# All input projections of a hybrid encoder layer in the first stage, the local attention between the steps of the scans, and the blocks of tokens taken middle first

## The chip, the cores and the metric

One core of one Trainium2 chip runs the whole layer in one launch. The metric is the device time of that launch in microseconds (us), the median over several runs. TensorE (PE in the rows) does the matrix products, VectorE (DVE), ScalarE (ACT) and GpSimd (POOL) the rest, and SyncE (SP) issues nearly all DMAs.

## The reference

One encoder layer on 2048 tokens of width 1024, in fp32. The normalised input goes through one projection whose columns feed three groups of heads; their outputs are joined and projected, and cross attention and a feed-forward layer follow.

```python
h = rmsnorm(x, norm_mix_w[l])
(na_q, na_k, na_v, ml_q, ml_k, ml_v, ml_o, ml_i, ml_f,
 gd_q, gd_k, gd_v, gd_z, gd_b, gd_a) = jnp.split(h @ w_in[l], IN_OFFSETS, axis=-1)
y_na = neighbourhood_attention(...)   # 6 heads of 64, windows of 8 x 16 on a 32 x 64 grid
y_ml = mlstm_mixer(...)               # 4 heads of 64, a scan over chunks in each direction
y_gd = gated_deltanet_mixer(...)      # 6 heads of 64, convolution, a scan in each direction
x = x + jnp.concatenate([y_na, y_ml, y_gd], axis=-1) @ w_out[l]
x = x + memory_cross_attention(rmsnorm(x, norm_xa_w[l]), rmsnorm(mem, norm_mem_w[l]), ...)
x = x + jnp.square(jax.nn.relu(rmsnorm(x, norm_ffn_w[l]) @ w_ff1[l])) @ w_ff2[l]
```

## The kernel before

Tokens go in four blocks of 512, activations lie transposed (features on partitions). A product with a weight tile of 128 columns (`gemm`, L1021, through `mm3`, L102) is 24 matmuls of 512 columns: eight slices of the 1024 features, each three times, since both operands are split into a high and a low part. I call such 24 matmuls a group. A weight tile is made by `wtile` (L980): a DMA of 512 KB, a rounding copy on ScalarE (L987, `whi`) and a subtraction on GpSimd (L989, `wlo`). The input projections are 120 groups: 36 for the delta rule's q, k, v (`gdn_in`, nine tiles per block), 4 for the gates, 24 for the mLSTM's q, k, v (`ml_in`), 32 for the attention's keys and values and the mLSTM's output gate (`na_kv`), 12 for the attention's queries (`na_q`), 12 for the delta rule's output gate (`gdn_z`).

The program is written as generators that a fixed order interleaves. A scheduler then arranges the instructions of each engine's queue; once built, each engine works through its queue in order. The stages are:

- **First stage** (`pass_a`, 0 to about 835 us). For each block: the nine tiles of `gdn_in`, each followed by a convolution over five tokens on VectorE (L299 to L311); then `gates`, and for each pair of chunks of 64 tokens `gram` (Gram matrices, decays, operands of the scan to DRAM). `inv` inverts the triangular matrices group by group: thirty pairs of VectorE instructions per direction (L495, L496), then rounds of small products (L524). Between these stand the mLSTM's projections and some of `na_kv`. Only two normalised blocks fit (`acta`, `actb`).
- **Scans** (`pass_b`, about 835 to 1290 us). The delta rule (`gdn_scan`, L653 to L689) and the mLSTM (`ml_scan`, L838 to L898), 16 steps each, both directions at once, with operands from DRAM loaded one step ahead. After each step one group of the projections that are left (`rest`) is put in. Blocks 0 and 1 have to be normalised again for this (`renorm`).
- **Attention** (`pass_c`, about 1290 to 1612 us). Sixteen blocks of 8 x 16 queries, six heads each (`na`, L948 to L976): scores, a bias and a maximum on VectorE (L952), exponentials on ScalarE (L953), transposes on TensorE (L957), the product with the values (L967). Scores take two banks of PSUM (`psn`), transposes two others (`pst`). The last projections and the other heads' outputs (`heads_out`, L707 to L727) stand between the blocks; the last five blocks stand between the tiles of the output projection's first block (`mixed`).
- **Rest**: output projection, cross attention, feed-forward layer.

The table below sets how many groups or steps go between two pieces; the line after it, in `pass_b`, is the place at which projections stand between the steps of the scans.

```python
B_FILL = 1
C_FILL = 3
NA_LATE = 11
OUTS = (0, 0, 0, 0, 1, 3, 3, 3, 3, 3, 0)
...
                    self.step(rest, B_FILL, L_B)
```

## Time and profile before

| | us |
|---|---|
| median of 3 runs | 3795.64 |
| the three runs | 3795.94, 3795.64, 3775.17 |
| span of the profiled execution, first to last instruction | 3789.0 |
| TensorE busy in the span | 3468.7 |
| VectorE busy | 1819.1 |
| GpSimd busy | 1601.0 |
| ScalarE busy | 1153.2 |

For the profiled execution only its span is known, 3789.0 us; two of the three timed runs lie 6.6 and 6.9 us above it, the third 13.8 us below. Busy time counts an instruction for as long as it runs, so TensorE's busy time is also longer where its clock is lower: the profile has a column with the clock granted to TensorE, where 1.00 is 2.4 GHz and 0.50 is 1.2 GHz. A busy time multiplied by the granted clock is what the same work would take at full clock; I call that warm work.

### The profile page before, as it was taken

To read this page: it belongs to the slowest core of one execution; us is meant where nothing else is said; L and a number is where in the kernel's file an instruction comes from. 1 tells how busy PE (TensorE), PEld (TensorE's weight loads), DVE (VectorE), ACT (ScalarE), POOL (GpSimd) and SP (SyncE) were. 2 spreads that over 40 slices of the span, in tenths; PEclk is the share of its full clock that TensorE was granted. 3 is DMA by queue.
4 is the path that set the end of the run, shared out by engine and by line. 5 is a ranking of instruction groups with operands and counts; after the bars stand their busy time and mean duration, and the time that the engine had idled before them with its cause. 6 is when DMAs were issued, how large, how long until landed. Compare 5 with 4: busy or idle time off the path is not lost.

```text
span 3789.0 us, 54073 instructions
## 1 busy us (share of the span) xinstructions
PE 3468.7 (92%) x21392; PEld 2774.0 (73%) x21392; DVE 1819.1 (48%) x3257; ACT 1153.2 (30%) x2015; POOL 1601.0 (42%) x947
## 2 busy tenths in 40 slices
PE   5878688888788889999999999999999999999998
PEld 4656566666666655588888887888888778888887
DVE  7697977625666644553443436222222352222224
ACT  3233232232323333544343344222222332222223
POOL 4455444554454531253535445333333453333333
PEclk9988888988899996999999999999999999999999
DMA  4546475678999565742233233111111141111112
GB/s 140 179 132 183 140 193 142 174 181 200 202 215 217 173 216 172 210 174 98 95 134 134 87 123 133 53 45 48 45 50 48 60 138 48 49 53 48 53 47 89
DMA packets 396663, 466.07 MB, mean 123 GB/s; under 512 B 151978, under 2 KB 296826, under 8 KB 393338
## 3 DMA queue, kind: packets, MB, share of 16 engines
q1 hardware_dynamic: 392794, 450.55, 41.2%
q0 software_dynamic: 3616, 12.06, 0.9%
q8 instruction: 169, 2.77, 0.3%
q14 instruction: 84, 0.69, 0.1%
HBM read 360.01 MB, written 102.50 MB: 122 GB/s over the span
## 4 chain that ended last, share of the span: by engine, by line
PE 52%; DVE 1%; ACT 1%; issue 1%; DMA 0%; POOL 0%; POOLq 0%; DVEq 0%; SPq 0%; ACTq 0%
PE psg L108 31%; PE psa L108 21%; PE psa L1180 0%; DVE nh L1005 0%; DVE ss L1016 0%; PE psm L88 0%; PE psm L99 0%; ACT whi L987 0%; DMA out_y<-nh 0%; DMA xb<-x_d 0%; POOL wlo L989 0%; DVE xb L1251 0%; ACT acta L1137 0%; ACT acta L1006 0%; ACT sqt L1015 0%
## 5 line engine op out<-in xcount | busy, mean ns | idle before, releaser
L989 POOL TENSOR_TENSOR wlo<-wraw,whi 128x1024 fp32r<-128x1024 f32 (+2 forms) x401 | 842.0, 2101 | 1294.1 <-ACT whi L987 1271.7
L108 PE MATMUL psg<-acta,whi 128*128 128x512 f32 x3008 | 975.3, 404 | 36.9 <-ACT pad L295 23.2
L108 PE MATMUL psg<-actb,whi 128*128 128x512 f32 (+2 forms) x2752 | 857.4, 393 | 36.8 <-DVE rt L613 10.2
L987 ACT CAST whi<-wraw 128x1024 fp32r<-128x1024 f32 (+2 forms) x417 | 373.5, 896 | 1192.3 <-PE psa L108 551.7
L108 PEld LDWEIGHTS psg<-acta,whi 128*128 128x128 f32 x3008 | 576.7, 194 | 169.2 <-ACT pad L295 25.2
L108 PE MATMUL psa<-ht,whi 128*128 128x512 f32 x2048 | 638.6, 395 | 0.6 <-ACT whi L987 0.5
L108 PEld LDWEIGHTS psg<-actb,whi 128*128 128x128 f32 (+1 forms) x2752 | 518.9, 193 | 148.2 <-ACT pad L295 11.2
L108 PE MATMUL psg<-acta,wlo 128*128 128x512 f32 x1504 | 602.5, 402 | 3.6 <-POOL wlo L989 3.6
L108 PE MATMUL psg<-actb,wlo 128*128 128x512 f32 (+2 forms) x1376 | 539.9, 393 | 27.9 <-POOL wlo L989 27.9
L108 PEld LDWEIGHTS psa<-ht,whi 128*128 128x128 f32 x2048 | 384.0, 188 | 95.1 <-ACT whi L987 1.5
L1229 DVE TENSOR_TENSOR fr<-fr 128x512 f32<-128x512 f32 x128 | 167.9, 1312 | 495.4 <-ACT fr L1228 495.4
L1242 DVE TENSOR_TENSOR xb<-psa,xb 128x512 f32<-128x512 f32 x256 | 175.6, 691 | 476.4 <-PE psa L108 476.3
L108 PE MATMUL psa<-ht,wlo 128*128 128x512 f32 x1024 | 401.0, 396 | 0.7 <-POOL wlo L989 0.7
L108 PEld LDWEIGHTS psg<-acta,wlo 128*128 128x128 f32 x1504 | 290.8, 193 | 67.6 <-POOL wlo L989 5.0
L108 PEld LDWEIGHTS psg<-actb,wlo 128*128 128x128 f32 (+1 forms) x1376 | 265.2, 193 | 86.5 <-POOL wlo L989 33.4
L1232 POOL TENSOR_TENSOR ht<-fr,ht 128x512 fp32r<-128x512 f32 x128 | 169.1, 1321 | 249.1 <-ACT ht L1231 247.8
L108 PEld LDWEIGHTS psa<-ht,wlo 128*128 128x128 f32 x1024 | 192.3, 188 | 47.5 <-POOL wlo L989 1.8
L1016 DVE TENSOR_TENSOR ss<-ss,sqt 128x512 f32<-128x512 f32 (+1 forms) x91 | 123.4, 1356 | 47.0 <-ACT sqt L1015 44.3
L308 DVE SCALAR_TENSOR_TENSOR acc<-pad,vecs,acc 128x512 f32<-128x512 f32 (+2 forms) x144 | 143.6, 1000 | 1.5 <-DVE sm L436 0.6
L1231 ACT CAST ht<-fr 128x512 fp32r<-128x512 f32 x128 | 79.4, 621 | 180.1 <-DVE fr L1229 180.0
L1228 ACT ACTIVATE fr<-psg 128x512 f32<-128x512 f32 x128 | 75.9, 593 | 132.3 <-PE psg L108 132.3
L495 DVE TENSOR_TENSOR tv<-x 72x30 f32<-72x30 f32 (+36 forms) x210 | 94.4, 470 | 2.0 <-DVE x L496 0.6
(376 smaller groups left out, 3982.3 us busy)
## 6 DMA issues: line engine op xcount, KB each, us to landing
wraw<-in_w_ff SPq DMA_DIRECT2D x72, 512.0 KB
wraw<-in_w_ff SPq DMA_DIRECT2D x144, 256.0 KB
wraw<-in_w_gd SPq DMA_DIRECT2D x36, 512.0 KB
sc_d<-sc SPq DMA_DIRECT2D x32, 576.0 KB
xt<-in_xT SPq DMA_DIRECT2D x16, 1024.0 KB
wraw<-in_w_out SPq DMA_DIRECT2D x32, 512.0 KB
wraw<-in_w_xq SPq DMA_DIRECT2D x32, 512.0 KB
wraw<-in_w_xo SPq DMA_DIRECT2D x32, 512.0 KB
```

The lines of the kernel that those rows point to most:

```text
L108: nc.tensor.matmul(out=out, lhsT=a(k), rhs=b(k), start=(i == 0), stop=(i == n - 1))
L308: V.scalar_tensor_tensor(out=acc[:, :n], in0=pad[:, p0 + j:p0 + j + n], scalar=cw(j), in1=acc[:, :n], op0=ALU.mult, op1=ALU.add)
L495: V.tensor_tensor(out=tv, in0=m[:, j + 1:32, j:j + 1].broadcast_to([2 * N, n, j]), in1=m[:, j:j + 1, 0:j].broadcast_to([2 * N, n, j]), op= ...
L987: nc.scalar.copy(out=hi, in_=raw)
L989: (lo_eng or nc.gpsimd).tensor_tensor(out=lo, in0=raw, in1=hi.bitcast(F32), op=ALU.subtract)
L1016: nc.vector.tensor_tensor(out=ss, in0=ss, in1=sq, op=ALU.add)
L1228: S.activation(out=r, in_=ps, func=AF.Relu)
L1229: V.tensor_tensor(out=r, in0=r, in1=r, op=ALU.mult)
L1231: S.copy(out=ht[:, 0], in_=r)
L1232: G.tensor_tensor(out=ht[:, 1], in0=r, in1=ht[:, 0].bitcast(F32), op=ALU.subtract)
L1242: V.tensor_tensor(out=xs[nb][:, j], in0=ps, in1=xs[nb][:, j], op=ALU.add)
```

## The change

All 120 groups of projections now stand in the first stage, which works on pairs of blocks: each weight tile of the pair is made once and used for both blocks (the first few tiles of `gdn_in`, `LEAD`, excepted, which are made for each block). Nothing is normalised twice. The scans' stage holds no projection any more: after each step stand three pieces (one block) of the attention, and from the tenth round on two pieces of `heads_out`, which now begins with the tokens in the middle, since both directions of the scans have passed them first. The attention's scores and transposes share two banks of PSUM (`psn`), and `heads_out` shares two with the mLSTM's scan (`psl`). The weights' and activations' memory (`gemm_pools`) is freed after the first stage, used by the attention and by `heads_out`, and taken anew for the rest. There the blocks go in the order 1, 2, 0, 3; the memory's norm and its first four tiles of keys stand ahead of the output projection, which no longer overlaps with the attention. Comments have gone, so line numbers differ by 8 to 19: the scans' L653, L672, L679, L686 are now L640, L659, L666, L673; the mLSTM's L849, L853, L878, L885 are L837, L841, L866, L873; the attention's L948, L957, L967, L972 are L936, L945, L955, L962; the heads' transposes L723 are L710; the projections' L108 is L95.

```diff
+LEAD = (4, 2)
+ORDER = (1, 2, 0, 3)
+KV_FIRST = 4
...
+            self.norm_in(1)
+            for pr in range(2):
+                bs = (2 * pr, 2 * pr + 1)
+                n = LEAD[pr]
+                for ct, blocks in [(c, bs[:1]) for c in range(n)] + [(c, bs) for c in range(n, 9)] + [(c, bs[1:]) for c in range(n)]:
+                    w = self.wtile(self.I["w_gd"][ct], KT, "w")
+                    for b in blocks:
+                        self.gdn_in(b, ct, w)
+                for b in bs:
+                    self.gates(b)
+                fill = chain(self.ml_in(bs), self.na_kv(bs), self.na_q(bs), *(self.gdn_z((b,)) for b in bs)) if pr == 0 else chain(self.na_kv(bs), self.na_q(bs), self.ml_in(bs), self.gdn_z(bs))
...
+            attn = self.na(pool("na", 2, side="right"))
             scan = self.gdn_scan(pool("scan", 2))
+            out = self.heads_out(pool("out", 2, side="right"))
...
+            for m in range(16 + LAG):
+                next(scan, None)
+                if m >= LAG:
+                    next(ml)
+                self.step(attn, 3)
+                if m - LAG >= 8:
+                    self.step(out, 2)
+            for _ in chain(attn, out):
+                pass
...
-        for t in range(16):
-            yield
+        yield
+        for t in (7, 8, 6, 9, 5, 10, 4, 11, 3, 12, 2, 13, 1, 14, 0, 15):
...
-                    tp = self.ntp.tile([P, 512], F32, name="pst")
+                    tp = self.nps.tile([P, 512], F32, name="psn")
...
-        blocks = sorted(NA_BLOCKS)
+        blocks = sorted(NA_BLOCKS, key=lambda k: (ORDER.index(k[0]), k[1]))
```

The first place is TensorE's queue in the middle of the scans. Before, a step of the delta rule (`pss`) and of the mLSTM (`psl`) has matmuls of the projections (`psg`, operands `acta`, `actb` and the weights' `whi`, `wlo`) in between.

```order
L885 MATMUL psl<-mr__10267,msc 64x65 x8
L653 MATMUL pss<-wp,kb 64x64 x24
L849 MATMUL psl<-mkq 64x64 x8
L853 MATMUL psl<-ident,mkq 64x128 x3
L672 MATMUL pss<-sc,wp 64x64 x12
L853 MATMUL psl<-ident,mkq 64x128
L108 MATMUL psg<-acta,wlo 128x512
L108 MATMUL psg<-acta,whi 128x512 x2
L108 MATMUL psg<-actb,whi 128x512
```

In the changed kernel a step looks like this, with the attention's scores and transposes (`psn`) and its products with the values (`psy`).

```order
L866 MATMUL psl<-mr__11299,msc 64x65 x8
L659 MATMUL pss<-sc,wp 64x64
L945 MATMUL psn<-ident,nas 96x128 x3
L945 MATMUL psn<-ident,nas 72x128
L936 MATMUL psn<-nak,naqb 128x360
L659 MATMUL pss<-sc,wp 64x64 x11
L873 MATMUL psl<-mr__11299,msc 64x65 x8
L866 MATMUL psl<-mr__11299,msc 64x65 x8
L955 MATMUL psy<-nap,nav 64x128
L666 MATMUL pss<-sc 64x64
L673 MATMUL pss<-sc 64x64
```

The projections have left this place, and every head's transposes (L945) now stand directly ahead of the next head's scores (L936).

The second place is TensorE's queue at the end of the attention. Before, matmuls of the output projection (`psg`) follow between its last heads.

```order
L948 MATMUL psn<-nak,naqb 128x288
L967 MATMUL psy<-nap,nav 64x128
L972 MATMUL pst<-ident,nsm 64x128 x6
L948 MATMUL psn<-nak,naqb 128x288
L967 MATMUL psy<-nap,nav 64x128 x5
L957 MATMUL pst<-ident,nas 96x128 x3
L948 MATMUL psn<-nak,naqb 128x288
L108 MATMUL psg<-acta,whi 128x512 x3
L108 MATMUL psg<-acta,wlo 128x512
```

In the changed kernel the attention is through by then; the last three steps of the mLSTM (`psl` from `msc`) and the last heads' transposes (`psl` from `ob`) stand alone, then come the memory's norm (`psm`) and the first product of the rest.

```order
L841 MATMUL psl<-ident,mkq 64x128 x4
L866 MATMUL psl<-mr__13869,msc 64x65 x8
L873 MATMUL psl<-mr__13869,msc 64x65 x8
L866 MATMUL psl<-mr__13869,msc 64x65 x8
L873 MATMUL psl<-mr__13869,msc 64x65 x8
L710 MATMUL psl<-ident,ob 128x128 x10
L866 MATMUL psl<-mr__14238,msc 64x65 x8
L873 MATMUL psl<-mr__14238,msc 64x65 x16
L710 MATMUL psl<-ident,ob 128x128 x10
L76 MATMUL psm<-ones,ss 128x1 x2
L86 MATMUL psm<-ident,rs 128x128 x2
L95 MATMUL psg<-actb,whi 128x256 x2
```

No dense product is left between the last heads; the first one of the rest stands behind all of them.

## Rows read from the trace of the kernel before

**Rows 1.** The page: span and busy time of TensorE and VectorE.

```profile
span 3789.0 us, 54073 instructions
...
PE 3468.7 (92%) x21392; PEld 2774.0 (73%) x21392; DVE 1819.1 (48%) x3257; ACT 1153.2 (30%) x2015; POOL 1601.0 (42%) x947
```

**Rows 2.** Busy time by stage, granted clock, DMA share (first stage, scans, attention).

```profile
core 0: us, PE busy (x) PEld busy (x) DVE busy (x) ACT busy (x) POOL busy (x), PEclk, DMA share, GB/s
0.00:835.00 835.00, 666.30 (x4456) 524.25 (x4457) 634.65 (x1287) 252.33 (x358) 412.36 (x219) 0.88 0.59 162
835.00:1290.00 455.00, 365.74 (x5375) 299.84 (x5373) 275.50 (x529) 134.12 (x259) 222.58 (x154) 0.90 0.87 204
1290.00:1612.00 322.00, 298.31 (x1768) 190.27 (x1768) 160.51 (x500) 133.31 (x359) 91.07 (x48) 0.86 0.64 198
```

**Rows 3.** The same stretches, the projections' matmuls (L108) alone.

```profile
0.00:835.00 835.00, 541.89 (x2032) 403.52 (x2033) 0.88 0.59 162
835.00:1290.00 455.00, 163.25 (x579) 112.10 (x577) 0.90 0.87 204
1290.00:1612.00 322.00, 73.86 (x285) 56.05 (x285) 0.86 0.64 198
```

**Rows 4.** The chain of waits: start, us, what; a group of 24 at full clock.

```profile
1907.14 5.49 PE psg L108 x24
```

**Rows 5.** Busy time by stretch: start, convolutions, twice Gram matrices with projections.

```profile
0.00:43.00 43.00, 16.18 (x53) 12.42 (x54) 23.81 (x43) 17.55 (x28) 19.87 (x24) 1.00 0.60 193
43.00:116.00 73.00, 56.33 (x231) 42.80 (x230) 67.87 (x97) 25.82 (x34) 33.03 (x14) 0.86 0.37 109
430.00:514.00 84.00, 64.24 (x340) 52.34 (x341) 64.19 (x157) 17.26 (x24) 36.63 (x13) 0.84 0.55 147
600.00:700.00 100.00, 89.71 (x842) 73.23 (x841) 65.60 (x162) 29.98 (x46) 41.44 (x20) 0.86 0.76 206
```

**Rows 6.** VectorE's groups in the first stage: busy us, mean ns, idle before.

```profile
L308 DVE SCALAR_TENSOR_TENSOR acc<-pad,vecs,acc 128x512 f32<-128x512 f32 (+2 forms) x144 | 143.6, 1000 | 1.5 <-DVE sm L436 0.6
L259 DVE TENSOR_REDUCE ss<-sq 128x256 f32<-128x1024 f32 x16 | 31.4, 1963 | 9.6 <-ACT sq L258 9.6
L311 DVE SCALAR_TENSOR_TENSOR acc<-th,acc 128x512 f32<-128x512 f32 (+2 forms) x36 | 30.0, 833 | 3.2 <-ACT th L310 3.1
L306 DVE TENSOR_SCALAR acc<-pad,vecs 128x512 f32<-128x512 f32 (+2 forms) x36 | 19.9, 552 | 3.8 <-DMA gd_c<-acc 2.9 <-ACT pad L295 0.8
L299 DVE COPY pad<-edge 128x4 f32<-128x4 f32 x27 | 19.2, 710 | 0.1
L303 DVE COPY edge<-pad 128x4 f32<-128x4 f32 x27 | 18.5, 685 | 3.2 <-ACT pad L295 3.1
```

**Rows 7.** Groups of instructions: VectorE's norm, attention's heads, heads' outputs on GpSimd.

```profile
L266 DVE SCALAR_TENSOR_TENSOR xt<-xt,vecs,psm 128x256 f32<-128x256 f32 x120 | 48.8, 471 | 33.0 <-PE psm L99 20.7 <-DMA xt<-in_xT 12.2
L948 PE MATMUL psn<-nak,naqb 64*128 64x360 f32 (+5 forms) x192 | 82.3, 594 | 0.1
L957 PE MATMUL pst<-ident,nas 128*96 128x128 f32 (+1 forms) x336 | 61.6, 308 | 3.6 <-ACT nas L953 2.7 <-ACT nay L974 0.9
L953 ACT ACTIVATE nas<-nas,nam 128x360 f32<-128x360 f32 (+5 forms) x96 | 57.8, 603 | 48.2 <-DVE nam L952 36.8 <-PE psm L723 3.5 <-DVE hss L715 3.4
L952 DVE CUSTOM_DVE_ANT_0 nas<-psn,nab 128x360 f32<-128x360 f32 (+5 forms) x96 | 51.1, 538 | 56.2 <-PE psn L948 50.0 <-PE pst L957 5.7
L707 POOL TENSOR_TENSOR ob<-ob 128x640 f32<-128x640 f32 x16 | 24.7, 1542 | 147.4 <-DMA ob<-ho_d 119.2 <-PE psn L948 18.8 <-PE pst L957 4.5
```

**Rows 8.** Ten-microsecond stretches of the attention: a wait, then a lower clock.

```profile
1370.00:1380.00 10.00, 10.00 (x72) 7.19 (x69) 3.80 (x14) 3.10 (x10) 3.40 (x2) 1.00 0.60 193
1410.00:1420.00 10.00, 7.06 (x41) 3.79 (x38) 4.76 (x20) 5.18 (x16) 4.99 (x3) 0.83 0.83 249
1420.00:1430.00 10.00, 10.00 (x40) 5.42 (x39) 3.22 (x11) 1.70 (x5) 1.95 (x1) 0.50 0.65 188
...
1450.00:1460.00 10.00, 9.72 (x73) 5.94 (x72) 6.16 (x19) 5.72 (x17) 3.46 (x2) 0.97 0.70 208
```

More of the change, by code (lines that the diff above doesn't have):

```diff
@@ L1 @@
 from contextlib import ExitStack
-from itertools import chain
+from itertools import chain, islice
 import numpy as np
@@ L167, in pass_a @@
             self.zero_w()
[L168 removed]
+            self.edges = [self.gp.tile([P, 9, 4], F32, name=f"edge{i}") for i in range(3)]
             with self.tc.high_priority(offset=500):
                 self.norm_in(0)
[L171 to L192 removed]
@@ L193, in pass_a @@
-            for _ in inv:
-                self.step(rest, I_FILL, L_A)
-        self.sp = None
-    def step(self, gen, n, late=0):
-        with self.tc.high_priority(offset=-late):
-            for _ in range(n):
-                next(gen, None)
-    def pass_b(self, rest):
+            self.norm_in(1)
[9 more added lines that the diff above has]
+                fill = chain(self.ml_in(bs), self.na_kv(bs), self.na_q(bs), *(self.gdn_z((b,)) for b in bs)) if pr == 0 else chain(self.na_kv(bs), self.na_q(bs), self.ml_in(bs), self.gdn_z(bs))
+                if pr == 0:
+                    self.grams((0, 1, 2), fill)
+                    inv = self.inv(0, (0, 1))
+                    self.steps(inv, fill, I_FILL, 1)
+                    self.grams((3, 4, 5, 6), fill)
+                    self.steps(chain(inv, self.inv(1, (0, 1))), fill, I_FILL)
+                    self.steps(fill, iter(()), 0, 34 - 14)
+                    self.norm_in(2)
+                    self.steps(fill, iter(()), 0)
+                    self.norm_in(3)
+                else:
+                    self.grams((15, 14, 13, 12, 11), fill)
+                    inv = self.inv(3, LAST[0])
+                    self.steps(inv, fill, I_FILL, 1)
+                    self.grams((7, 8, 9, 10), fill)
+                    self.steps(chain(inv, self.inv(2, (0, 1)), self.inv(3, LAST[1], late=LATE_POOL)), fill, I_FILL)
+                    self.steps(fill, iter(()), 0)
@@ L205, in pass_b, with grams, steps, step @@
+        self.sp = None
+    def grams(self, ts, fill):
+        for t in ts:
+            self.gram(t)
+            self.step(fill, G_FILL)
+    def steps(self, gen, fill, n, most=None):
+        for _ in gen if most is None else islice(gen, most):
+            self.step(fill, n)
+    def step(self, gen, n):
+        for _ in range(n):
+            next(gen, None)
+    def pass_b(self):
         with ExitStack() as st:
```

188 lines of the change are left out of this document (58 added, 130 removed).

## The prediction

> **What bounds the kernel now.** I read the page first: TensorE is busy 92% of the span, no other engine half of it [rows 1]. That is an average, so I then took the busy times by stage [rows 2]. Up to 1612 us TensorE is busy 1330 of 1612 us and its clock is at 0.86 to 0.90 of full; behind that it is nearly always busy, and the change leaves the work there as it is. So only the three stages up to 1612 us matter. Third, I took the projections alone [rows 3]: 2032 of their matmuls run in the first stage, 579 between the scans, 285 around the attention (14 of these are already the output projection). At full clock 24 of them, one group, take 5.49 us [rows 4].
>
> In warm work (busy time by clock) the stages hold 666.3 x 0.88 = 586, 365.7 x 0.90 = 329 and 298.3 x 0.86 = 257 us, together 1172 of 1612 us. The other 440 us are waits and a low clock: 249, 126 and 65 us. The change can only win from these, so the question is what the new order does to each of the three.
>
> **First stage: 835 to 957 us.** It gains 850 matmuls (579 + 285 - 14), 35.4 groups, 35.4 x 5.49 = 194 us of warm work: 780 in all. What it loses I take piece by piece.
> - Start: the first 43 us hold 16 us of TensorE's work [rows 5] and stay.
> - Convolutions: VectorE needs per tile 4 x 1.00 + 0.83 + 0.55 + 0.71 + 0.69 = 6.8 us [rows 6], more than a group's 5.49, so it sets the pace here; the stretch from 43 to 116 us shows it, VectorE 67.9 of 73 us busy [rows 5]. Eighteen tiles of a pair are 122 us, the norm of a block 2 x (2 x 1.96 + 8 x 0.47) = 15.4 [rows 6, 7] and some small ones: 139 us per pair, 278 for both, over 40 groups of TensorE's work. In the second pair the norm of block 3 needs `actb` free and comes a few us late: 8.
> - The rest holds 780 - 16 - 220 = 544 us of warm work: 80 groups, 16 Gram matrices, the inverses. From 600 to 700 us the kernel before did such a mixture, five Gram matrices in 100 us, and lost 100 - 89.7 x 0.86 = 23 us [rows 5], or 4.6 for each. Sixteen lose 74. The stretch from 430 to 514 us, where tiles serve one block only, did worse: 64.2 x 0.84 / 84 = 0.64. Ends: nothing lost, 544; 0.64 as there, 850. I take 544 + 74 = 618, the denser row, since its weight tiles serve two blocks like the new ones.
> - End: the last rounds of the inverses stand alone: 10.
>
> Sum 43 + 278 + 8 + 618 + 10 = 957 us, 122 more than before. The 18 weight tiles and four norms that are dropped cost no time where they stood: GpSimd was busy 412 of 835, 223 of 455 and 91 of 322 us [rows 2]. Their DMAs (18 x 512 KB and four blocks of x) leave the shared queue of SyncE.
>
> **Between the stages: 10 us.** The attention's keys lie where weight tiles lay, so their loads, and all that SyncE has queued behind them, start only when the last group is done. The kernel before shows no such hand-over; the nearest are the inverses' last rounds, which may cover it (0), and the start of the program, which needed most of 43 us [rows 5]. I take 10.
>
> **Scans with attention: 777 to 628 us.** Scan work is (365.7 - 163.3) x 0.90 = 182 us warm, attention with the heads' outputs (298.3 - 73.9) x 0.86 = 193 [rows 2, 3]. I counted pieces in the changed queue of TensorE: when the delta rule's last step is issued, 11.5 of 16 blocks of attention and 10 of 16 steps of the mLSTM are through.
> - Up to there: 160 us of scan and 139 of attention, 299 warm, where before 329 went in 455 us. The DMA engines were the fuller resource, busy 0.87 [rows 2], and the scans' loads stay; the attention's keys and biases replace weights and x. I take 455 + 10. At a mean clock of 0.80 that is 374 us of matmuls and 91 of waits, as many waits as before (455 - 366 = 89). Ends: 410, if heads fill half of the waits, and 545, if the clock sinks to 0.60.
> - 4.5 blocks of attention that are left: a head is a chain of scores, maximum, exponential and three or four transposes, 0.59 + 0.54 + 0.60 + 3.5 x 0.31 = 2.8 us [rows 7], with four hand-overs 3.4. In the new queue the next scores stand behind these transposes, so nothing overlaps: 6 x 3.4 = 20 us a block, 92 in all, and 16 for mLSTM steps that don't fit between: 108 (75 if they overlap as before, 130 at the lower clock).
> - Three mLSTM steps and the last heads, with nothing beside them: 55 us. Before, GpSimd waited up to 119.2 us in 11 waits for these heads' loads [rows 7], about 11 each, under the attention's cover; the cover is gone. Ends 35 and 75.
>
> **Sum.** +122 + 10 + 465 + 108 + 55 - 777 = -17 us on a span of 3789. The median of the runs is 6.6 us above that span, so I forecast 3795.6 - 17 = 3779 us. A measurement of this kernel tells about 1% from no change, 38 us; this is inside.
>
> **The clock.** In the attention a wait of 2.9 us (1410 to 1420) is followed by some 30 us at 0.50, the lower level, in which 40 instead of 72 matmuls ran in 10 us though TensorE had no pause [rows 8]. The Trainium skill ("TensorE: Matmul & The Clock Gate", "Loop structure matters more than you think") says the same as a rule: keep matmuls back to back, since waits between bursts let the engine go cold. By this rule the middle stage, which loses its runs of dense matmuls, goes the way of the first rival.
>
> **The rivals.**
> 1. *The clock stays low between the scans* (slower). Waits of a few us at every step, no projections to bring the clock back. For: rows 8. Against: with scan work alone between projections it was 0.90 [rows 2]. At a mean of 0.60, half of the waits vanish behind slower matmuls: 299 / 0.60 + 45 = 543, 76 / 0.60 + 10 = 137, and 55: 735 us. Then +122 + 10 + 735 - 777 = +90: 3886 us. With everything else as forecast it decides from a mean clock of about 0.77 down, where the stage passes 645 us.
> 2. *Both halves fill their gaps* (faster). The first stage reaches 0.97 on its 544 us (561, so 900 us, +65), because no projection waits for its weights any more; the heads fill half of the scans' waits at 0.88 of full clock, so that only the loads hold them (430), then 95 and 50: 575 us. For: two independent streams, and the attention alone kept TensorE busy 298 of 322 us [rows 2]. +65 - 202 + 10 = -127: 3669 us.
> 3. *The DMA engines become the bound.* Before, 0.87 x 455 + 0.64 x 322 = 602 us of full DMA work [rows 2]. Of the 156 MB moved there (204 x 455 + 198 x 322 [rows 2]) about 28 leave: some 22 weight tiles of 0.5 MB, 8 MB of x, 35 results of 0.25 MB; at the 322 GB/s of a full queue at the start (193 / 0.60 [rows 5]) that is 87 us. 515 us at the 0.87 reached are 592, and 55 for the end: 647 us, +122 + 10 - 130 = +2: 3798 us.
>
> **How the numbers follow.** Forecast 0.36, with its own range from 3740 to 3830 (the first stage 30 us either way, the middle 30); clock 0.24; both filled 0.32; DMA 0.08. Faster by over 1% is the second rival and a sixth of the forecast: 0.38. Slower is the first: 0.24. The rest is 0.38. The range from 3680 to 3890 reaches to both outer cases and leaves about half of each tail of theirs out; the parts' ends (the first stage from 883 to 1189, the middle from 520 to 750) would allow more, but not all at once.
>
> **What would show it.** In the profile of the changed kernel: the last projection of the first stage at about 945 us (850 or 1050 would break the first term); VectorE over 0.9 busy in the two stretches of convolutions; the delta rule's last step some 475 us later; a mean clock of 0.80 up to there; then 15 to 25 us per block of attention, and some 55 us nearly without TensorE ahead of the first product of the rest, at about 1595 us. If the clock there lies at 0.65 or less, the first rival holds; if TensorE waits less than 50 us between the scans' steps, the second; if the DMA share lies above 0.95 throughout, the third. I am wrong if the time leaves 3740 to 3830, or if the rest behind the attention takes other than its 2170 us.

## The result, and the profile after

| | before | changed |
|---|---|---|
| median of the runs, us | 3790.69 (4 runs, 3775.17 to 3795.94) | 3925.97 (4 runs, 3921.89 to 3929.86) |
| ratio, 95% interval | 1 | 1.0371 (1.0345 to 1.0396) |
| span of the profiled execution, us | 3789.0 | 3928.0 |
| end of the first stage, us | 835 | 960 |
| end of the attention and the heads, us | 1612 | 1752 |

The change makes the kernel 3.7% slower. The forecast was 3779 us, within 1% of before, and the range ended at 3890.

The page of the changed kernel, which answers to [rows 1]: TensorE is now busy 89% of the span.

```profile
span 3928.0 us, 53839 instructions
...
PE 3493.0 (89%) x21360; PEld 2812.2 (72%) x21360; DVE 1742.0 (44%) x3193; ACT 1129.1 (29%) x1989; POOL 1483.8 (38%) x921
```

Busy time by stage, as in [rows 2]. The stages are now three: all projections; scans with attention and heads; the rest.

```profile
core 0: us, PE busy (x) PEld busy (x) DVE busy (x) ACT busy (x) POOL busy (x), PEclk, DMA share, GB/s
0.00:960.00 960.00, 818.07 (x5115) 656.29 (x5116) 595.69 (x1236) 263.43 (x379) 362.83 (x214) 0.93 0.52 141
960.00:1752.00 792.00, 538.36 (x6511) 394.63 (x6507) 409.84 (x1033) 239.15 (x591) 250.34 (x186) 0.71 0.70 181
1752.00:3928.00 2176.00, 2136.58 (x9740) 1761.32 (x9740) 736.42 (x924) 626.48 (x1020) 870.58 (x522) 0.99 0.24 78
```

The rest takes 2176 us; before it was 3789 - 1612 = 2177. So the whole loss lies ahead of it: the first stage is 125 us longer, and the middle, from which 35 groups of projections were taken, is not shorter than the two stages it replaces (792 against 777). In warm work it did shrink, to 538.4 x 0.71 = 382 us, close to the forecast's 299 + 76; the other 410 us, waits and a low clock, are what grew (before: 777 - 329 - 257 = 191).

The same view of the middle's four parts: up to the delta rule's first step, its 16 steps, the rest of the attention, the end.

```profile
960.00:1021.00 61.00, 27.12 (x278) 18.73 (x276) 12.14 (x28) 10.62 (x26) 3.65 (x2) 0.54 0.84 214
1021.00:1516.00 495.00, 388.75 (x5297) 294.13 (x5298) 282.07 (x672) 177.31 (x444) 168.95 (x127) 0.78 0.79 193
1516.00:1650.00 134.00, 92.50 (x655) 57.73 (x655) 64.64 (x194) 33.98 (x87) 37.24 (x28) 0.65 0.57 170
1650.00:1752.00 102.00, 29.98 (x291) 24.04 (x287) 51.00 (x141) 17.24 (x34) 40.50 (x30) 0.53 0.37 114
```

Against the forecast these are 61 for 10, 495 for 465, 134 for 108 and 102 for 55 us. The last row is the plainest: 102 us in which TensorE has 30 us of work.

The stores of the two scans say what the end waits for: the delta rule's 16 (L676), then the mLSTM's (L886) ahead of 1516 us and behind it (count, duration, first and last start).

```profile
L676 POOL DMA_DIRECT2D ho_d<-o x16: 668/682/713, 1051.8 to 1520.9; - x16
...
L886 POOL DMA_DIRECT2D ho_d<-mo x10: 656/672/785, 1107.4 to 1455.5; - x10
...
L886 POOL DMA_DIRECT2D ho_d<-mo x6: 671/677/691, 1518.2 to 1717.9; - x6
```

When the delta rule is through, the mLSTM has done 10 of 16 steps, as counted in the queue beforehand; the other six take 200 us more, and the heads' outputs of the outer blocks wait for them. Before, the mLSTM's last store started 26 us behind the delta rule's (L689, then L898):

```profile
L689 POOL DMA_DIRECT2D ho_d<-o x16: 668/673/781, 890.4 to 1291.7; - x16
L898 POOL DMA_DIRECT2D ho_d<-mo x16: 676/777/790, 902.0 to 1318.2; - x16
```

The longest waits of the middle stage in the changed kernel: who waited for whom, us in total, times, longest.

```profile
POOL me L827 <- DVE me L826: 162.8, 11, 24.6
ACT nas L941 <- DVE nam L940: 144.1, 59, 13.6
POOL sc L632 <- DMA wp<-w_d: 79.6, 2, 70.7
DVE me L826 <- DMA me<-mx_row: 77.1, 13, 13.0
```

`me` is an operand of the mLSTM, loaded into a single buffer; `wp` is the delta rule's, and its one wait of 70.7 us is the start of the scans.

### The profile page after: what moved, and what is told of

The parts are those of the page before. It is cut to its first block, busy times and chain, and to the rows that moved or that the text cites. A ratio compares the mean times of both kernels' runs of the same rounds, so it can differ in the third digit from the quotient of the medians.

```text
span 3928.0 us, 53839 instructions
## 1 busy us (share of the span) xinstructions
PE 3493.0 (89%) x21360; PEld 2812.2 (72%) x21360; DVE 1742.0 (44%) x3193; ACT 1129.1 (29%) x1989; POOL 1483.8 (38%) x921
## 4 chain that ended last, share of the span: by engine, by line
PE 61%; DMA 10%; DVE 7%; issue 3%; SPq 2%; ACT 2%; POOL 1%; DVEq 0%; POOLq 0%; ACTq 0%
PE psg L95 34%; PE psa L95 20%; DVE acc L295 1%; DMA me<-mx_row 1%; PE psn L936 1%; DMA mkq<-mlc_d 1%; DMA ge<-g_row 1%; DVE tv L482 1%; PE psn L945 1%; DVE x L483 1%; PE psy L955 1%; DMA nab<-in_nab 1%; DMA wp<-w_d 1%; DMA sc<-v_d 1%; DMA ob<-ho_d 1%
## 5 line engine op out<-in xcount | busy, mean ns | idle before, releaser
L979 POOL TENSOR_TENSOR wlo<-wraw,whi 128x1024 fp32r<-128x1024 f32 (+1 forms) x383 | 777.4, 2030 | 1400.2 <-ACT whi L977 1362.2
L95 PE MATMUL psg<-acta,whi 128*128 128x512 f32 (+1 forms) x3008 | 956.4, 399 | 4.3 <-ACT acta L1118 3.2
L95 PE MATMUL psg<-actb,whi 128*128 128x512 f32 (+1 forms) x2752 | 840.4, 387 | 43.2 <-ACT actb L260 17.5
L95 PEld LDWEIGHTS psg<-acta,whi 128*128 128x128 f32 (+1 forms) x3008 | 570.6, 191 | 127.6 <-ACT acta L1118 3.9
L95 PE MATMUL psa<-ht,whi 128*128 128x512 f32 x2048 | 638.8, 395 | 0.8 <-ACT whi L977 0.8
L95 PEld LDWEIGHTS psg<-actb,whi 128*128 128x128 f32 x2752 | 514.2, 191 | 151.2 <-ACT actb L260 18.1
L95 PE MATMUL psg<-acta,wlo 128*128 128x512 f32 (+1 forms) x1504 | 595.7, 397 | 1.1 <-POOL wlo L979 1.1
L95 PE MATMUL psg<-actb,wlo 128*128 128x512 f32 (+1 forms) x1376 | 531.8, 387 | 3.2 <-POOL wlo L979 3.2
L95 PEld LDWEIGHTS psa<-ht,whi 128*128 128x128 f32 x2048 | 384.0, 188 | 95.3 <-ACT whi L977 1.6
L95 PE MATMUL psa<-ht,wlo 128*128 128x512 f32 x1024 | 400.7, 396 | 0.5 <-POOL wlo L979 0.5
L95 PEld LDWEIGHTS psg<-acta,wlo 128*128 128x128 f32 (+1 forms) x1504 | 286.8, 191 | 63.7 <-POOL wlo L979 2.3
L95 PEld LDWEIGHTS psg<-actb,wlo 128*128 128x128 f32 x1376 | 262.9, 191 | 55.4 <-POOL wlo L979 4.9
L95 PEld LDWEIGHTS psa<-ht,wlo 128*128 128x128 f32 x1024 | 192.2, 188 | 47.3 <-POOL wlo L979 1.7
L945 PE MATMUL psn<-ident,nas 128*96 128x128 f32 (+1 forms) x336 | 75.1, 352 | 52.3 <-ACT nas L941 52.2
```

What stands on the lines that cost most here:

```text
L95: nc.tensor.matmul(out=out, lhsT=a(k), rhs=b(k), start=(i == 0), stop=(i == n - 1))
L945: nc.tensor.transpose(out=tp[:n, P * j:P * j + P], in_=s[:, kt * j:kt * j + n], identity=self.ident)
L979: (lo_eng or nc.gpsimd).tensor_tensor(out=lo, in0=raw, in1=hi.bitcast(F32), op=ALU.subtract)
```

## The experiments

Letters name the theories as the expectations do: A, a cold clock; B, waits for loads, with B1 (single buffers and arrival) and B2 (throughput); C, the projections stood in free time; D to H as they come. "Middle" is the time from 960 us to the start of the rest (the span less 2177). Each time is compared by its ratio to the kernel before, run beside it.

### Was the work that left the middle worth anything there?

`bshort`, the kernel before:

```diff
-            put(self.gemm(w, self.acts[b % 2]), slice(512 * b, 512 * b + 512))
+            put(self.gemm(w, self.acts[b % 2], nk=self.nkp), slice(512 * b, 512 * b + 512))
```

`nkp` is 8 in the first stage and 1 behind it.

> The kernel before, in which every projection group that stands in the scans and around the attention has 3 of its 24 matmuls (one of eight k-tiles; its results are therefore not the reference's); weight loads, casts and stores stay. So some 850 x 7/8 = 744 matmuls, 744 x 5.49 / 24 = 170 us of warm TensorE work, are gone from the 777 us between 835 and 1612 us, nothing else. Theory C (what the change moved out stood in time that the scans and the attention leave anyway, so taking it away saves nothing, and the clock falls instead): the stage lasts 740 us or more, its granted clock falls from 0.88 to 0.75 or less, in all 3750 or more. The forecast's reckoning, in which the middle shrinks by what leaves it: 777 - 150 = 627, in all 3640 us or less.

3747.31 us, ratio 0.9905 (0.9880 to 0.9931). Both stages, then the scans alone:

```profile
835.00:1570.00 735.00, 537.59 (x6336) 389.68 (x6337) 437.07 (x1026) 267.82 (x613) 315.33 (x204) 0.76 0.81 213
844.00:1263.00 419.00, 277.25 (x4725) 236.47 (x4725) 282.07 (x527) 143.84 (x264) 236.04 (x158) 0.75 0.94 227
```

Of 170 us of warm work, 36 come back; the clock falls from 0.88 to 0.76. Theory C is near (its bound of 3750 is missed by 3 us, its 740 by 5, its clock of 0.75 by 0.01), the forecast's 3640 is 107 us off: four fifths of these matmuls stood in time that the scans and the attention leave anyway. The groups' loads, casts and stores stayed in this run; in `pairs`, below, they are gone too, and scans and attention take 733 us (3866.4 - 2177 - 956), 44 less than the 777 of before. This is the first reason of the miss: the forecast let the middle shrink by 149 us.

### Is it the clock?

`pss2`, a control, takes one bank from the delta rule's scan; `fill16` puts useless matmuls into that bank:

```diff
-            self.sps = pool("pss", 3, space=PSUM)
+            self.sps = pool("pss", 2, space=PSUM)
...
-                self.step(attn, 3)
+                for _ in range(3):
+                    self.step(attn, 1)
+                    for _ in range(16):
+                        self.nc.tensor.matmul(out=fp, lhsT=fx[:, 0], rhs=fx.rearrange("p a b -> p (a b)"), start=True, stop=True)
```

> Control for the next run: the changed kernel with two instead of three PSUM banks for the delta rule's scan. All theories: within 1% of the changed kernel (3926 us), so 3890 to 3965; a larger loss would say that the third bank carries the scan.

> The changed kernel with two banks for the delta rule's scan and, in the freed bank, 16 matmuls of 128x512 without use behind each of 48 attention pieces (three per scan step): 768 matmuls, as many as the 32 projection groups that the change took out of the middle, 32 x 5.49 = 176 us of warm work. Theory A (cold clock): the clock of the middle rises from 0.71 to 0.9 or more, its own matmuls shrink from 538 us busy to about 382 / 0.9 = 424, and the stage lasts no longer than without them: 780 us or less, in all at or below 3926 us. Theory B (waits for loads): the clock rises too, but the stage stays at 790 to 830 us, in all 3925 to 3965, because the useless matmuls stand in time that TensorE waited anyway. If TensorE itself is the bound: 792 + 176 = 968 us, in all about 4100.

`pss2`: 3928.67 us, ratio 1.0366 (1.0325 to 1.0407), no difference. `fill16`: 3999.20 us, 1.0560 (1.0514 to 1.0605), 71 us more (51 pieces ran, so 816 matmuls instead of 768). Its middle:

```profile
960.00:1825.00 865.00, 693.93 (x7310) 509.25 (x7311) 411.23 (x1031) 240.80 (x592) 252.32 (x185) 0.83 0.63 166
```

The useless matmuls were busy 223 us of these 694, so the kernel's own work took 471 instead of 517 in `pss2`: the clock rose from 0.72 to 0.83 and gave 46 us of matmuls back. The stage grew by 79 us all the same. So a warmer clock bought in this way doesn't pay, and less than half of TensorE's added time fell on the path. Neither A nor B was met: A expected no loss, B at most 40.

`lessattn` leaves out two thirds of the attention's work on the engines:

```diff
             for hp in range(3):
+                if hp > 0:
+                    if hp < 2:
+                        yield
+                    continue
```

> The changed kernel in which the attention computes two of its six heads (the results of the others are therefore wrong); all its loads and stores stay. About 150 x 2/3 = 100 us of warm TensorE work, 140 us at the clock of 0.71, and the same share of the attention's work on VectorE and ScalarE are gone from the middle stage. Theory A or TensorE's own chain of heads holds the middle: 792 - 140 = 650 us or less, in all 3785 or less. Theory B (loads hold it): 740 us or more, in all 3875 or more.

3876.20 us, ratio 1.0233 (1.0192 to 1.0275), 52 us less. The middle:

```profile
960.00:1700.00 740.00, 390.23 (x5622) 314.22 (x5622) 359.14 (x883) 167.20 (x372) 251.10 (x184) 0.66 0.74 191
```

148 us of TensorE's busy time are gone, the stage is 52 us shorter, and its scans (1020 to 1507 us) as long as before: 487 us for 495. The attention's work on TensorE, VectorE and ScalarE isn't what paces the steps; B's 740 is met to the microsecond.

### Order and queues

`seq` drops `self.step(attn, 3)` from the loop; `queue` issues the attention's DMAs from ScalarE's queue (`nc.scalar.dma_start` in `na`).

> The changed kernel with the local attention behind the scans instead of between their steps (heads' outputs still between the last scan steps); nothing else moves. In the changed kernel the middle stage, from the last projection to the end of heads and attention, lasts 792 us. Theory A (the middle is held by the granted clock, 0.71, because no projections stand there any more): two thin streams one after the other leave TensorE colder still, the stage grows to 850 us or more, in all 3985 us or more. Theory B (the middle is held by waits for loads and by the in-order SyncE queue, and the two streams hold each other up): scans alone 61 + 16 x 26 = 477, attention alone 16 x 17 = 272, end 20, so 769 or less, in all 3900 us or less. If the two streams do fill each other's gaps as forecast: over 900, in all over 4030.

> The changed kernel with the local attention's loads and stores issued by ScalarE's DMA queue instead of SyncE's. Theory B (SyncE's queue takes its issues in order, so the attention's loads that wait for TensorE and VectorE, 24.0 and 11.8 us in the listed waits, hold back the loads of the scans): the DMA pieces of the chain (me 35, mkq 33, ge 30 us) shrink, the stage falls from 792 to about 740 us, in all about 3875. Theory A (cold clock): within 10 us of 3926. If ScalarE's own work is held back by issues that wait, the ACT waits (nas 69 us) grow and the time rises by 20 us or more.

`seq`: 3901.13 us, ratio 1.0296 (1.0250 to 1.0342), 28 us less than the changed kernel, middle 761, within the 769 of theory B; so the two streams do not fill each other's gaps. The scheduler still pulled some seven blocks of attention between the steps. `queue`: 3942.92 us, 1.0408 (1.0370 to 1.0445), no gain. The delta rule ends at 1607 us instead of 1516, the attention at 1708 instead of 1647, the stage only 12 us later (804). That SyncE's queue holds the loads back falls as the main cause. Nor does the delta rule set the end: in `pss2` it ends 45 us later than in the changed kernel, and the stage does not.

### The loads: waits or throughput?

`bufs` gives three operands two buffers:

```diff
-            ge = pool.tile([P, 2, 6, 64], F32, name="ge", bufs=1)
+            ge = pool.tile([P, 2, 6, 64], F32, name="ge", bufs=2)
...
-            kq = pool.tile([P, 2, 4, P], F32, name="mkq", bufs=1)
-            e = pool.tile([P, 2, 4, 64], F32, name="me", bufs=1)
+            kq = pool.tile([P, 2, 4, P], F32, name="mkq", bufs=2)
+            e = pool.tile([P, 2, 4, 64], F32, name="me", bufs=2)
```

> The changed kernel with two buffers instead of one for three of the scans' loaded operands (ge, mkq, me), which stand for 30, 33 and 35 us of the chain in the middle stage. If the wait is for a free buffer (theory B1): these pieces mostly go, the stage falls from 792 to about 720 us, in all about 3855. If the DMA engines' throughput or the place in SyncE's queue holds them (B2), or the clock (A): within 15 us of 3926.

3892.56 us, ratio 1.0274 (1.0225 to 1.0324), 37 us less: half of what B1 expected, more than the others allow.

`noload` loads six operands at the first step alone; `loadidle` and `loadkept` add as many bytes again that nobody reads. One of the six loads, in the three runs:

```diff
-                nc.sync.dma_start(out=qe[SR[d]], in_=self.gd_c[0:3, :, P * t:P * t + P].rearrange("c (h e) l -> e (c h) l", h=2))
+                if m == 0:
+                    nc.sync.dma_start(out=qe[SR[d]], in_=self.gd_c[0:3, :, P * t:P * t + P].rearrange("c (h e) l -> e (c h) l", h=2))
+                elif m > 1:
+                    nc.sync.dma_start(out=nc_d[2 * m + d, :, :, :, 0:P], in_=self.ho_d[m - 2, 0:64, :, 256:640].rearrange("p d (a l) -> p d a l", l=P))
```

(`noload` without the `elif`; `loadidle` with the old source at every step and, behind the first, a target in DRAM that nobody reads; `loadkept` as shown.)

> The changed kernel with six operands of the scans loaded at the first step alone and used again at every later step (ge, qe, mqe, mge, mkq and me; results are therefore not the reference's): 33 of the 143 MB of the middle stage are gone, with the waits for them; matmuls and the other engines' work stay. Theory B (loads hold the middle: DMA share 0.79 between the scan steps): of 0.70 x 792 = 554 us of DMA work 33 / 143, 128 us or more, go, and the stage falls from 792 to 690 us or less, in all 3825 or less. Theory A (the clock holds it): 770 us or more, in all 3905 or more.

> As the run without the six loads (its results are not the reference's either), but the six loads of every later step are still issued, from the same places in SyncE's queue and with the same bytes per row, into DRAM that nobody reads: the DMA engines have their work back, nobody waits for it. Theory B2 (the DMA engines' throughput and SyncE's queue hold the middle): most of the 100 us that leaving the loads out gained is lost again, 3890 us or more. Theory B1 (the waits for single buffers hold it): as without the loads, 3826 us, at most 3850.

> As the run without the six loads (noload: 3826 us, 110 MB in the middle stage instead of 143; its results are not the reference's either), but at every later step as many bytes in rows of 512 to 1536 bytes are copied, on the same queue, from the delta rule's output of two steps before into DRAM that nobody reads, so that they can't run ahead of the scan. B1 (the waits for the loads and their single buffers): 3850 us or less. B2 (throughput of the DMA engines and the queue): 3890 us or more, DMA share of the middle 0.70 or more.

| | us | ratio, 95% | middle, us |
|---|---|---|---|
| noload | 3825.80 | 1.0107 (1.0056 to 1.0158) | 679 |
| loadidle | 3807.84 | 1.0062 (1.0036 to 1.0089) | 666 |
| loadkept | 3840.45 | 1.0130 (1.0081 to 1.0179) | 705 |

What the DMA engines moved in the middle stage, in the changed kernel, `noload`, `loadidle` and `loadkept`, in this order:

```profile
DMA packets 138648, 143.23 MB, mean 181 GB/s; under 512 B 12828, under 2 KB 121164, under 8 KB 138060
```

```profile
DMA packets 91344, 109.73 MB, mean 160 GB/s; under 512 B 9932, under 2 KB 76028, under 8 KB 91004
```

```profile
DMA packets 98227, 119.40 MB, mean 180 GB/s; under 512 B 10892, under 2 KB 80828, under 8 KB 97649
```

```profile
DMA packets 137285, 140.98 MB, mean 200 GB/s; under 512 B 12636, under 2 KB 121740, under 8 KB 136716
```

The first row of `loadidle` shows why that run decides nothing: loads that nothing holds were issued ahead of the stage, only 10 of the 33 MB stayed. `noload` meets B's 690 us for the middle and misses its 3825 by a microsecond. In `loadkept` the bytes and the packets are those of the changed kernel within 2%, and the stage still ends 87 us earlier; by the ratio 91 of the 100 us of `noload` remain, and B1's bound of 3850 is met. So over the whole stage the six loads cost mostly by being waited for, not by the DMA engines' throughput. Up to the delta rule's last step alone it is otherwise. These are its 16 steps in `noload` and `loadkept`:

```profile
1014.00:1444.00 430.00, 363.48 (x5342) 277.14 (x5342) 300.32 (x700) 179.71 (x451) 177.43 (x131) 0.85 0.62 161
1019.00:1495.00 476.00, 388.75 (x5529) 294.58 (x5530) 318.50 (x746) 187.89 (x473) 188.36 (x140) 0.84 0.79 216
```

Of the 65 us that `noload` takes from the 495, 46 are lost again once the bytes move, though not for quite the same work: 12 steps of the mLSTM and 156 of 192 matmuls of scores are through by then, against 11 and 146 in `noload`, 10 and 142 in the changed kernel. In this stretch the bytes may well count; most of the gain of `loadkept` comes behind it. That `bufs` got only 37 says that a second buffer for three of them is part of it, the arrival and the other three the rest; which share each has wasn't tried.

### The three steps of the change one after the other

`pairs2`: two blocks per weight tile and no norm twice, the rest of the order as before. `pairs`: all projections ahead as well. The core of both:

```diff
+            for pr in range(2):
+                bs = (2 * pr, 2 * pr + 1)
...
+                    w = self.wtile(self.I["w_gd"][ct], KT, "w")
+                    for b in blocks:
+                        self.gdn_in(b, ct, w)
...
-            fill = chain(*([] if ZB else [self.gdn_z((0, 1))]), self.renorm((2, 3)), self.na_q((2,)), self.gdn_z((2, 3)), self.na_q((3,)))
+            fill = chain(self.na_q((2, 3)), self.gdn_z((2, 3)))
```

In `pairs2` the results of the 26 late groups go to buffers that lie where the inverses' and the scans' tiles lay, which holds these groups back; in `pairs` nothing holds them.

> The first part of the change alone, built into the kernel before: two blocks per weight tile in the first stage and no norm computed twice; the scans, then the attention, in the old order, with 94 projection groups ahead of the scans, 16 between their steps and 10 around the attention (85, 24 and 11 before). If TensorE's work between the scan steps is nearly free, as the run with an eighth of it says, and the cost of the change lies in putting it all ahead: first stage 960 - 26 x 5.49 / 0.9 = 801 us, scans 440, attention 300, together 1541 instead of 1612, in all about 3720 (3690 to 3760). If instead the first stage of the change is the costly part, it is 860 or more here and the time 3790 or more.

> As pairs2, but with the projections of the second pair free to run as early as they can: all 120 groups stand ahead of the scans as in the changed kernel, and scans and attention follow one another as before, with nothing between. Between this run and pairs2 only the place of 26 groups differs. Theory C: first stage 960, scans 420 (held by their loads, as in the run with an eighth of the projections), attention 280, together 1660 instead of 1612: in all about 3840 (3810 to 3870), 120 us over pairs2. If putting them ahead costs nothing: within 20 us of pairs2.

`pairs2`: 3839.63 us, ratio 1.0163 (1.0135 to 1.0191); `pairs`: 3870.55 us, 1.0233 (1.0201 to 1.0265). So the three steps cost about 62, 26 and 52 us (1.0163, then 1.0233, then 1.0371): no part of the change wins, and each expectation of a gain was wrong. For `pairs2` the other branch came true (first stage 860 us or more, 3790 or more); `pairs` met neither, 26 to 31 us over `pairs2` where theory C expected 120. `pairs2`, the last inverses, the scans, the attention:

```profile
800.00:935.00 135.00, 42.52 (x860) 38.15 (x861) 60.61 (x180) 27.66 (x46) 44.08 (x65) 0.50 0.56 105
948.00:1331.00 383.00, 304.87 (x5051) 253.73 (x5045) 258.27 (x508) 116.08 (x234) 196.70 (x143) 0.91 0.90 211
1358.00:1646.00 288.00, 267.99 (x1581) 164.00 (x1582) 137.91 (x446) 119.62 (x342) 63.58 (x35) 0.85 0.59 182
```

`pairs`, the scans, the attention:

```profile
982.00:1393.00 411.00, 245.05 (x4631) 223.25 (x4631) 245.38 (x487) 103.26 (x210) 161.01 (x135) 0.72 0.71 177
1423.00:1690.00 267.00, 249.66 (x1447) 144.79 (x1446) 134.78 (x455) 114.32 (x336) 56.86 (x33) 0.80 0.62 185
```

In `pairs2` a hole of 135 us opens in which TensorE works 42 us at the lower clock: the inverses of the last two blocks now end together, with nothing beside them. In `pairs` TensorE is busy 122 of the same 135 us, and its scans begin only 34 us later (982 for 948), though 26 groups more, 143 us of warm work, stand ahead. The scans of `pairs2`, with 16 groups between the steps, take 383 us at a clock of 0.91; those of `pairs`, with none, take 411 at 0.72.

`pairs3` and `pairs3b` share tiles in the first pair alone and project blocks 2 and 3 as before; they differ in the groups between the scan steps (16 and 22).

> Two blocks per weight tile in the first pair of blocks alone; blocks 2 and 3 are projected one after the other as before, so that the inverses of block 2 stand under the convolutions of block 3; no norm computed twice; 100 projection groups ahead of the scans, 16 between their steps, 4 around the attention. In pairs2 TensorE worked 29 of the 100 us from 800 us on, in the last inverses, and its scans took 383 instead of 424 us. Theory F (late inverses cost pairs2 its time): the scans begin at 890 us or earlier instead of 948, in all 3765 (3735 to 3790), at or below the kernel before. Theory G (sharing the tiles is at fault): 3815 or more.

> As pairs3 with 94 groups ahead of the scans and 22 between their steps. If groups between the scan steps are nearly free, the scans begin 20 to 30 us earlier than in pairs3 and end as early or earlier: 3735 to 3775, at most 10 us over pairs3. If the scans are as full with 16 groups as they can be: 20 us or more over pairs3.

3833.89 us, ratio 1.0129 (1.0104 to 1.0155), and 3836.35 us, 1.0153 (1.0119 to 1.0187). The scans still begin at 948 us in both, so theory F fails as it was put; the hole is there too (TensorE 42 and 20 us busy from 800 to 900). `pairs3b` stays within 10 us of `pairs3`, at a time far above the 3735 to 3775 that was expected. G's bound of 3815 is passed, but sharing was not separated from what goes with it, the 40 groups of the first pair ahead of blocks 2 and 3. What makes this first step slow stays open; that 94 groups or 100 ahead give the same time says that it is not TensorE's work there.

The scans of `pairs3` and `pairs3b`, and those of the kernel before from the delta rule's first step to its last (24 groups):

```profile
948.00:1346.00 398.00, 315.73 (x5049) 257.88 (x5048) 256.01 (x508) 116.92 (x234) 194.94 (x143) 0.88 0.89 202
948.00:1349.00 401.00, 337.23 (x5161) 274.18 (x5156) 259.27 (x498) 121.34 (x241) 204.25 (x146) 0.93 0.87 207
856.00:1280.00 424.00, 344.45 (x5145) 283.17 (x5140) 270.11 (x516) 127.19 (x247) 211.39 (x147) 0.90 0.87 203
```

So with 16 to 24 groups between the steps the clock is 0.88 to 0.93 and the scans take 383 to 424 us; with none (`pairs`) or an eighth of the matmuls (`bshort`) it is 0.72 and 0.75, and they take 411 and 419. In these runs the clock follows the projections, the length of the scans hardly does: projections there are nearly free, and that they shorten the scans isn't shown.

### Do the scans wait for these loads in any order?

`pairs_idle` is `pairs` with the edit of `loadidle` (and the input's buffer freed at the end of the first stage, for room).

> The run pairs (all projections ahead, then scans, then attention) with the edit of loadidle: six loads of every later scan step go to DRAM that nobody reads (its results are not the reference's). In the changed kernel, with the attention between the scan steps, this gained 118 us. Theory D (the waits for single-buffered operands grow because two streams stand in one SyncE queue): here at most 50 us are gained, 3820 or more. Theory E (the scans wait for these loads in any order): 90 us or more are gained, 3780 or less.

3795.88 us, ratio 1.0027 (1.0010 to 1.0044), 78 us under `pairs`: between the two bounds. The profile says more: the scans took 298 us instead of 411, and began 58 us later (1040 instead of 982), with idle loads ahead of them.

```profile
1040.00:1338.00 298.00, 211.02 (x4669) 193.19 (x4668) 256.26 (x498) 102.68 (x212) 171.44 (x133) 0.85 0.56 142
```

So the scans wait for the six loads in either order; the window is 113 us shorter, with fewer bytes to move in it, as in `loadidle`. Theory D as it was put (50 us at most) falls, theory E (90 or more) isn't met. Whether the interleaving adds to these waits stays open: the same edit gained 118 us in the changed kernel, and here the idle loads ahead of the scans may be what made them begin later.

### The shared PSUM banks

Before, the heads' outputs were transposed in a bank apart from the scans' (`psm`, L723), behind the scans; the change puts them into the two banks of the mLSTM (`psl`, L710). `ownbank` takes that back:

```diff
-            self.sps = pool("pss", 3, space=PSUM)
+            self.sps = pool("pss", 2, space=PSUM)
+            self.hps = pool("psh", 1, space=PSUM)
...
-                ps = self.lps.tile([P, 512], F32, name="psl")
+                ps = self.hps.tile([P, 512], F32, name="psh")
```

`ownbank_bufs` adds the edit of `bufs`.

> The changed kernel with a PSUM bank of its own for the transposes of the heads' outputs, taken from the delta rule's scan (two instead of three, which alone cost nothing in pss2); before the change these transposes had a bank of their own too (psm), in the changed kernel they share psl's two with the mLSTM. By order 15 of 16 mLSTM steps then stand ahead of the delta rule's last (11 in the changed kernel). Theory H (the shared banks hold the mLSTM back, and its last steps stand alone at the end): the 102 us behind the attention's last scores shrink to 50 or less, in all 3880 or less. Otherwise (the mLSTM lags because of VectorE, GpSimd or its loads): within 15 us of 3926.

> ownbank with two buffers for ge, mkq and me as in bufs. Theory H and B1 together, if their gains add: 46 or more and 33 us, in all 3845 or less; still above the kernel before, since the first stage costs 122 us more. If both gains are the same wait: within 10 us of ownbank.

`ownbank`: 3854.68 us, ratio 1.0199 (1.0185 to 1.0213), 65 us less. `ownbank_bufs`: 3838.22 us, 1.0159 (1.0145 to 1.0173), 15 more: the gains add in part. The stores of `ownbank`:

```profile
L677 POOL DMA_DIRECT2D ho_d<-o x16: 663/679/751, 1060.1 to 1589.5; - x16
L887 POOL DMA_DIRECT2D ho_d<-mo x16: 663/682/781, 1109.8 to 1600.5; - x16
```

Its middle, and its end, which answers to the row 1650 to 1752:

```profile
960.00:1677.00 717.00, 527.80 (x6514) 386.16 (x6511) 417.07 (x1033) 237.33 (x590) 256.22 (x184) 0.73 0.78 200
...
1600.00:1680.00 80.00, 57.70 (x233) 33.63 (x232) 40.14 (x108) 27.97 (x66) 29.39 (x22) 0.56 0.57 181
```

The mLSTM now ends 11 us behind the delta rule, not 197: its last store starts 117 us earlier, the delta rule's 69 us later. The attention runs to 1655 us and the rest starts at 1677. Behind the attention 22 us are left instead of 102: theory H. The edit moves nothing else, and the bank taken from the delta rule cost nothing (`pss2`). But the engines' queues are arranged anew with it: when the delta rule's last step ends, the mLSTM has now stored 14 of its 16 steps, and 10 in the changed kernel. Whether the shared banks cost by the order that was built or by waits while it runs wasn't separated. No version was found that beats the kernel before; `ownbank_bufs` is the best of the changed order and still 1.6% slower, and its middle of 699 us, 78 under the 777 of before, doesn't make up for the 125 us by which the first stage is longer.

## Why the prediction was wrong

**First stage, 835 to 957.** The number was right, 960, with 35 more groups in it. By its parts, convolutions of the first pair, what follows, convolutions of the second pair, what follows:

```profile
43.00:182.00 139.00, 111.51 (x484) 86.78 (x483) 120.03 (x167) 41.88 (x59) 46.14 (x18) 0.90 0.35 100
182.00:516.00 334.00, 293.57 (x2043) 238.23 (x2042) 189.45 (x463) 91.01 (x128) 116.37 (x51) 0.93 0.58 152
516.00:645.00 129.00, 109.97 (x471) 85.79 (x470) 108.26 (x161) 33.79 (x50) 39.14 (x15) 0.92 0.25 74
645.00:960.00 315.00, 288.53 (x2079) 234.47 (x2078) 153.52 (x405) 80.02 (x118) 141.08 (x107) 0.93 0.64 167
```

The convolutions took 268 us for 278 + 8, the rest 649 for 618 + 10. VectorE was busy 0.86 and 0.84 of the convolutions (120.0 of 139, 108.3 of 129 us), not over 0.9, so the pace there was set less by it than reckoned. And the reason behind the sum, TensorE's work that is added, is only part of it: `pairs2`, with 26 of these groups left out of the stage, begins its scans at 948 us. How much of the 125 us is the price of the groups, and how much that of the stage's new order, stays open; that the sum came out is in part luck.

**Between the stages, 10.** Mis-sized: 61 us from the last projection to the delta rule's first step. The place was right: SyncE's queue stands at the attention's keys (L896) until the last group is done, and the scan's first load (L623) follows 24 us later.

```profile
959.61 1.27 SPq L896 DMA_DIRECT2D nak<-nac_d  x3
...
962.38 0.52 SPq L908 DMA_DIRECT2D nab<-in_nab  x1
...
974.20 4.43 SPq L914 DMA_DIRECT2D nav<-nav_d  x3
...
983.29 2.49 SPq L623 DMA_DIRECT2D wp<-w_d  x1
```

But the queue alone is not it: with the attention's loads on ScalarE's queue the scan's first load started at 981 us and the first step came at 1021 as well; what holds them there wasn't separated. In `pairs`, where the attention's loads come later and the scan's first load starts at 811 us, the first step came 26 us behind the last projection (956, 982).

**Up to the delta rule's last step, 465.** 495 us. The counts held (142 of 192 matmuls of scores, 11.8 blocks; 10 mLSTM steps), the warm work held (388.75 x 0.78 = 303 for 299) and the clock nearly (0.78 for 0.80). The waits are 106 for 91. So this term was nearly right by itself. What was wrong is the thought behind the middle as a whole, 628 us for 777, that stages from which projections leave give their time back: `bshort` shows 36 of 170 us. The steps do depend on the six loads (430 us without them), but by which share through waits isn't shown for this stretch (476 in `loadkept`).

**Attention that is left, 108; last mLSTM steps and heads, 55.** 134 and 102. This is the step that failed most, 73 us of the 154 by which the middle missed. It counted three mLSTM steps for the end, which is what the trace shows, and priced them as work without cover; it did not ask why the mLSTM, which kept pace before, had fallen six steps behind. The answer stood in the diff (`psm` to `psl`) and was not priced: a bank of their own for the heads' transposes brings 65 us back.

**The sum.** The forecast's -17, 3 more for the first stage, and 51 + 30 + 26 + 47 = 154 for the middle make 140 us; the spans differ by 139. By the runs the same loss reads: 125 for the first stage, 44 given back by the projections that left the middle (`pairs`, 733 for 777) where the forecast had 149, and 59 lost by the attention between the steps (792 for 733). With a bank of their own for the heads' transposes the same order takes 717 us, 16 less than the attention behind the scans.

**The rivals.** The first came nearest (3886), in part by luck: the clock was 0.71 over the middle, under its 0.77, but 0.78 between the steps, where its mark was 0.65; 0.53 to 0.65 were seen at the start of the scans and behind the delta rule, where TensorE waits. And raising the clock by idle work cost 71 us. The Trainium skill's rule on the loop ("TensorE: Matmul & The Clock Gate", "Loop structure matters more than you think") agrees with the clock in these runs (0.91 in the scans of `pairs2`, 0.72 in those of `pairs`), but the time did not follow it: 383 to 424 us with projections, 411 without, and `fill16` lost 71 us at a clock of 0.83. The second rival was wrong on both counts. The third named the right resource: the loads did hold the stage, but mostly by waits, and the DMA share was 0.79 between the steps, not above 0.95. On queues the trace agrees with the Trainium skill ("Trainium Kernel Development and Optimization", "Key Constraints"), by which issuing from several engines saves only the sequencer's issue time: `queue` gained nothing (3942.92 us for 3925.97). On banks, the Trainium skill ("Perfetto Trace Analysis", "Matmuls") asks to rotate independent groups of matmuls through different banks, so that emptying one overlaps the next group. The 65 us of `ownbank` point the same way; whether they come from such overlap isn't shown.

## What to carry to other kernels

Matmuls that stand between the steps of a loop that waits for something else can be nearly free there, as here (36 of 170 us), and moving them elsewhere then saves little: before such a move, shorten them in place and see what comes back. When two streams are interleaved, list the pools that they come to share; a stream that falls behind another shows in the first and last start of its stores, which no busy share tells. Whether loads cost by bytes or by waiting is seen only when the same bytes move with nobody waiting, and such a run must be shown to have moved them in the stage.

## What the runs showed of the hardware that was not expected

With the DMA engines at a share of 0.79 and 193 GB/s in the scan steps of the changed kernel, they looked like the bound; yet `loadkept` moved as many bytes within 2% (141 MB) in a stage of 705 instead of 792 us, at 200 instead of 181 GB/s, once nobody waited for about a fifth of them. A high share was therefore no proof that the stage is held by its bytes; for the 0.94 and 227 GB/s in the scans of `bshort` this was not tried. And the granted clock rose in a stage when waits for loads were taken away: with nearly the same matmuls (4631 and 4669), 0.72 in the scans of `pairs` and 0.85 in those of `pairs_idle`.
